# Convolution pieces in a queue beside a matrix product, a state-space stream in smaller pieces, and another division of PSUM

## The chip, the cores and the metric

The kernel runs on one core of a Trainium2 chip. Its engines work from queues of their own, each in order: TensorE (PE for its products, PEld for its weight loads), VectorE (DVE), ScalarE (ACT), GpSimd (POOL) and SyncE (SP), which here issues nearly all DMAs. The metric is the device time of one execution in microseconds (us), the median of several runs.

## The reference

Two blocks follow each other, with 2048 tokens of width 1024. The first holds attention, a short convolution and a recurrent time mix. The second, in which the change lies, projects tokens and 256 context tokens with one matrix, and mixes them by a pooling branch, a state-space stream (SSD) and a gated delta-rule stream (GDN), each in two directions over chunks of 64 tokens; a product, a router and 16 experts come behind. Cut to what matters:

```
pc, pl = split(h_ctx @ w_in), split(h_lat @ w_in)           # the second input product
# SSD: xbc = silu(conv5(xbc) + b);  xs, B, C = split(xbc);  a = decay of each step
y_intra = ((C @ B^T) * decay) @ (xs * dt)                   # within a chunk
states  = (B * exp(a_last - a))^T @ (xs * dt)               # of a chunk
s       = s * chunk_decay + states                          # from chunk to chunk
y_inter = (C * exp(a)) @ s_start
y       = rms_norm((y_f + y_b + d_skip * xs) * silu(z))
# GDN: qkv = silu(conv5(qkv));  tm = inverse(I + strict_lower((k*beta) @ k^T * decay))
u, w    = tm @ (v * beta), tm @ (k * beta * exp(g))
v_new   = u - w @ s;  o = (q*exp(g)) @ s + attn @ v_new;  s = s * g_end + k_end^T @ v_new
```

## The kernel before

`Mid.run` holds the second block up to its output product. In `In2.run` the input product goes over jobs of 128 columns. A job has for every 512 tokens 24 matmuls (three for each of eight pieces of the inner dimension, `mm3`, line 66), then a copy out of PSUM (line 1160) and, for the parts gate and z, four transposes (line 1166). It runs twice: over the first 1024 tokens and the context, and over the other 1024 tokens ("the second run", 25 jobs: dab 1, qkv 9, pool 2, xbc 7, gate 3, z 3).

Beside the second run stand, each emitted whole or by shares between jobs: `Decay.run` (decay tables, some vector work), `ConvG.group` for nine groups of GDN channels (per group five pieces: four taps on VectorE, line 1209, a last multiplication, line 1212, transposes, line 1220; then norms and transposes back), `Pool.run` (eight pieces: sums on GpSimd, line 1390, on VectorE, line 1392, one matmul, line 1398, a copy by ScalarE, line 1400), and `ConvS.run`, the convolution of SSD, seven groups for each stretch of tokens in `CSP`.

Then comes the mixed stage. `Gdn.run` is 18 steps, a new one every `GDN_EVERY` = 15 rounds of `timed`, its front part `GDN_LEAD` = 16 rounds earlier. A step is: front (`ld`, `gram`), the inverse (`TriInv`: first part on VectorE, lines 256 to 296, second part five rounds of small products `tri`, line 318, each copied out of PSUM before the next), and `back` (`big` twice, line 1767, then `chain`, lines 1793 and 1796, which carries the state). Each round of GDN also calls `feed(RATE3)`, which draws the other stream: the rest of `ConvS` and then `Ssd.run`, first backwards (d = 1), then forwards (d = 0), by pairs of chunks. A chunk ("unit" below) is four matmuls: `y` from the state (line 1916) and `st` (line 1922), with the state scaled by GpSimd (line 1927) and `st` added by VectorE (line 1928). Forwards, a pair also has the products within its chunks ("intra part"): `g`, two `ld` (line 1950) with exponentials by ScalarE (line 1951), products of these by VectorE and GpSimd (lines 1952, 1954, 1958), `i` (line 1963), the sums and the gate (line 98).

The program's text gives priorities only: a scheduler orders every engine's queue by them and by when it believes operands and buffers free. PSUM has eight banks; in the mixed stage three tiles of two banks are shared by all of GDN's products, and two of one bank by the other stream:

```
pg, pq = k.psum(eg, "gp", 3, **R), k.psum(eg, "sp", 2, **L)
RATE3 = 0.35
```

Of the kernel before, what the change touches and what calls it, by code (L numbers as in the profile page):

```python
# [1125 lines left out]
class In2:  # L1126
# [22 lines left out]
    def block(self, wts, segs, hh, hl, dst=None, tok=None):  # L1149
# [4 lines left out]
        for c0, n, p0 in segs:  # L1154
            for u in range(0, n, 512):
                un = min(512, n - u)
                ps = self.pp.tile([128, 512], F32, tag="ps", name="ps")
                k.mm3(ps[:m, :un], [(wh[:, c], wl[:, c], hh[:, c, c0 + u:c0 + u + un], hl[:, c, c0 + u:c0 + u + un]) for c in (ROT if m == 36 else range(8))])
# [12 lines left out]
    def run(self, order, segs, hh, hl):  # L1171
# [15 lines left out]
        for j, (part, i, _, sg, kw) in enumerate(jobs):  # L1187
            nxt = self.weights(*jobs[j + 1][2]) if j + 1 < len(jobs) else None
            self.block(w, sg, hh, hl, **kw)
            w = nxt  # L1190
            yield part, i

# [43 lines left out]
class ConvG(Conv):  # L1236


    def __init__(self, k, a, es, p2, gT, gtm, psf, psf2, **kw):
# [4 lines left out]
        self.cw = self.weights(a["gdn_conv_w_2"][0], 9, w1)  # L1244

    def group(self, g):
# [21 lines left out]
        for p0, n in PIECES:  # L1268
            s0 = p0 + (4 if p0 == T else 0)
            y = self.taps(self.cw[:, g], None, pad[:, s0:s0 + n + 4], n)  # L1270
            t, m = p0 // 128, n // 128
            self.turn(tm[:, t:t + m].rearrange("p t c -> p (t c)"), lambda j: y[:, j * 128:j * 128 + 128], m)
            if g >= 6:
                continue
            sq = wp.tile([128, 8, 64], F32, tag="sq", name="sq")[:, :2 * m]
            tv = th[:, 2 * t:2 * t + 2 * m]
            G_.tensor_tensor(out=sq, in0=tv, in1=tv, op=ALU.mult)
            V.tensor_reduce(out=ss[:, 2 * t:2 * t + 2 * m], in_=sq, axis=AX.X, op=ALU.add)
# [3 lines left out]
        rs = k.rstd(wp, ss, 36, 1.0, 1e-6, "l2")  # L1282
        if g < 3:
            V.tensor_scalar(out=rs, in0=rs, scalar1=0.125, scalar2=None, op0=ALU.mult)
        for p0, n in PIECES:
            t, m = p0 // 128, n // 128
            tv = th[:, 2 * t:2 * t + 2 * m]
            G_.tensor_tensor(out=tv, in0=tv, in1=bc(rs[:, 2 * t:2 * t + 2 * m].unsqueeze(2), [128, 2 * m, 64]), op=ALU.mult)
            y = wp.tile([128, 512], F32, tag="yn", name="yn")
            self.turn(y[:, :n], lambda j: tm[:, t + j, :], m, self.psf2)  # L1290
            nc.sync.dma_start(self.gT[g * 128:g * 128 + 128, p0:p0 + n], y[:, :n])
        if g >= 3:
            store(0, 0, 18)


class ConvS(Conv):
# [12 lines left out]
    def run(self, pieces):  # L1309
        for p0, n in pieces:  # L1310
            for g in range(7):
                self.piece(g, p0, n)
                yield

    def piece(self, g, p0, n):
# [14 lines left out]
        if g < 5:  # L1330
            m = n // 128
            tm = wp.tile([128, 4, 128], F32, tag="tm", name="tm")[:, :m]
            self.turn(tm.rearrange("p t c -> p (t c)"), lambda j: y[:, j * 128:j * 128 + 128], m)
            nc.sync.dma_start(self.sst[p0:p0 + n, g * 128:g * 128 + 128].rearrange("(t p) c -> p t c", p=128), tm)
# [125 lines left out]
class Decay:  # L1460


    def __init__(self, k, a, es, p2, **kw):
        nc = k.nc
        self.k, self.a, self.p2, self.nc = k, a, p2, nc
        self.srow = k.dram([NCH, 12, 64], "srow")
# [7 lines left out]
    def run(self, psf, **kw):  # L1474
# [5 lines left out]
        with ExitStack() as e2:  # L1480
# [36 lines left out]
            dt = softplus(nc, wp, xr[:, 0:2, :], [NP, 2, 256], "sp")  # L1517
            beta = wp.tile([NP, 256], F32, tag="beta", name="beta")
# [30 lines left out]
            v.tensor_tensor(out=e2b, in0=e2v[:, 1, :], in1=beta, op=ALU.mult)  # L1549

# [11 lines left out]
            for n, src in back.items():  # L1562
                if n not in self.cols and n not in self.g:
                    continue
                ps = psf("t")
# [24 lines left out]
            nc.sync.dma_start(gt.rearrange("p s c d h -> p (s c d h)"), gdc.rearrange("c d -> (c d)").partition_broadcast(128))  # L1590
            for c in range(4):
                self.by_step(self.g["gdc"], c, gt[:, :, c].rearrange("p s d h -> p d s h"))

# [265 lines left out]
class Ssd:  # L1859


    def __init__(self, k, a, m, dec, es, bcT, sst, ztok, stok, psf, **kw):
# [4 lines left out]
        self.w2 = k.pool(es, "ss2", 2, **kw)  # L1867
        self.yb = [k.dram([128, 384], f"yb{p}") for p in range(16)]
# [12 lines left out]
    def run(self):  # L1881
# [12 lines left out]
        for d in (1, 0):  # L1894
            S = None
            order = ([16, 17] if d == 0 else [17, 16]) + (list(range(16)) if d == 0 else list(range(15, -1, -1)))
            for p in order:
                lat = p < 16
                t0 = p * 128
                xb = w2.tile([128, 640], F32, tag="xb", name="xb")  # L1900
                nc.sync.dma_start(xb, self.sst[t0:t0 + 128, :])
                xs = h6(xb[:, 0:384])
                xw = w2.tile([128, 6, 64], F32, tag="xw", name="xw")
                G_.tensor_tensor(out=xw, in0=xs, in1=bc(dec.col("sw", p, d).unsqueeze(2), [128, 6, 64]), op=ALU.mult)
                if lat:
# [6 lines left out]
                for i, u in enumerate((0, 1) if d == 0 else (1, 0)):  # L1912
                    rows = slice(u * 64, u * 64 + 64)
                    if lat:
                        for g in range(2):
                            nc.tensor.matmul(py[rows, g * 192:g * 192 + 192], bct[:, 2 + g, rows], S[:, g * 3:g * 3 + 3, :], start=True, stop=True)
                        if i == 1:
# [13 lines left out]
                if not lat:  # L1931
                    continue
# [544 lines left out]
```

## Time and profile before

| what | value |
|---|---|
| median of three runs | 4551.71 us (4546.35 to 4559.96) |
| profiled execution | 4546.18 us, its span 4544.4 us |
| busy in the span | PE 85%, PEld 71%, DVE 61%, ACT 43%, POOL 30% |
| mean granted clock of TensorE | 0.927 of full speed |
| second run of the input product | from about 2240 to 2683 us of the span |
| mixed stage | from about 2690 to 3497 us |

Busy time is the sum of an engine's instructions; PE's are modelled at their ends, so that a busy share near 90% does not mean that no time is left. A wait row names the instruction that waited and what released it.

### The profile page before, as it was taken

How to read it: one execution, taken by the hardware profiler on the slowest of the kernel's cores; microseconds unless marked ns; L12 is line 12 of the kernel's file. 1: busy time of each engine (PE TensorE's matmuls, PEld its weight loads, DVE VectorE, ACT ScalarE, POOL GpSimd, SP SyncE). 2: the span in 40 equal slices, each digit the busy share in tenths (PEclk: the TensorE clock that was granted, in tenths of full speed). 3: DMA queues.
4: the chain of work that ended last, by engine and by line, in shares of the span. 5: the costliest groups of instructions: out<-in, count | busy, mean ns of one | idle time of the engine just before them, and what ended most of it. 6: DMA issues, size and time to landing. Idle time of an engine off the chain costs nothing. (4 is left out here: it accounts for less than half of the span.)

```text
span 4544.4 us, 69094 instructions
## 1 busy us (share of the span) xinstructions
PE 3884.3 (85%) x25852; PEld 3231.2 (71%) x25852; DVE 2791.8 (61%) x5608; ACT 1960.8 (43%) x3984; POOL 1341.9 (30%) x1138
## 2 busy tenths in 40 slices
PE   7899999899788879899987858888885993799993
PEld 5688777677577767788765647777775783689993
DVE  7644555664588855323289776666776446866664
ACT  3134434343678742233336545455555221244442
POOL 2222222322311112221145444445553431011110
PEclk9999999899899989999989989998888996899997
DMA  6722322421412133334444654433333534577776
GB/s 224 233 85 83 96 91 85 120 69 57 124 48 69 49 107 130 128 104 142 109 112 143 171 155 121 130 99 99 105 109 111 175 119 135 176 232 234 232 228 203
DMA packets 551829, 595.65 MB, mean 131 GB/s; under 512 B 98310, under 2 KB 435378, under 8 KB 551494
## 3 DMA queue, kind: packets, MB, share of 16 engines
q1 hardware_dynamic: 538182, 547.17, 39.1%
q0 software_dynamic: 13312, 44.06, 4.0%
q8 instruction: 205, 3.36, 0.3%
q14 instruction: 130, 1.06, 0.1%
HBM read 426.62 MB, written 164.20 MB: 130 GB/s over the span
## 5 line engine op out<-in xcount | busy, mean ns | idle before, releaser
L66 PE MATMUL ps<-hh,wh 128*128 128x512 f32 (+2 forms) x1992 | 806.4, 405 | 4.9 <-ACT st L1160 3.4
L66 PE MATMUL ps<-hh,wl 128*128 128x512 f32 (+2 forms) x1992 | 783.4, 393 | 0.0
L66 PE MATMUL ps<-hl,wh 128*128 128x512 f32 (+2 forms) x1992 | 783.3, 393 | 0.0
L73 POOL TENSOR_TENSOR wl<-raw,wh 128x1024 fp32r<-128x1024 f32 (+1 forms) x136 | 320.8, 2361 | 820.3 <-ACT wh L72 785.8
L72 ACT CAST wh<-raw 128x1024 fp32r<-128x1024 f32 (+2 forms) x236 | 320.0, 1365 | 443.1 <-PE g L66 156.7
L66 PEld LDWEIGHTS ps<-hh,wh 128*128 128x128 f32 (+1 forms) x1992 | 380.4, 191 | 89.4 <-issue 6.1
L66 PEld LDWEIGHTS ps<-hh,wl 128*128 128x128 f32 (+1 forms) x1992 | 379.4, 190 | 85.1 <-issue 2.5
L66 PEld LDWEIGHTS ps<-hl,wh 128*128 128x128 f32 (+1 forms) x1992 | 381.3, 191 | 77.5 <-issue 2.2
L1209 DVE SCALAR_TENSOR_TENSOR y<-pad,cw,y 128x512 f32<-128x512 f32 (+2 forms) x348 | 263.6, 794 | 103.7 <-ACT y L1207 93.2
L66 PE MATMUL g<-xh,wh 128*128 128x256 f32 x1024 | 291.3, 286 | 17.2 <-ACT xh L2323 17.2
L66 PE MATMUL g<-xl,wh 128*128 128x256 f32 x1024 | 290.3, 284 | 1.6 <-DVE idx L2305 1.6
L66 PE MATMUL g<-xh,wl 128*128 128x256 f32 x1024 | 291.3, 285 | 0.0
L73 DVE TENSOR_TENSOR wl<-raw,wh 128x2048 fp32r<-128x2048 f32 (+1 forms) x100 | 225.1, 2263 | 105.2 <-ACT wh L72 104.8
L66 PE MATMUL o<-wh,mh 128*128 128x512 f32 x512 | 207.5, 406 | 12.7 <-DMA mraw<-mixT 12.7
L801 DVE TENSOR_REDUCE nm<-s 128x1 f32<-128x512 f32 (+3 forms) x320 | 186.0, 604 | 51.6 <-PE s L796 33.0
L2390 POOL DMA_INDIRECT x<-y,idx x32 | 63.3, 1980 | 520.1 <-DVE y L2388 452.8
L66 PEld LDWEIGHTS g<-xh,wh 128*128 128x128 f32 x1024 | 195.0, 191 | 18.5 <-ACT xh L2323 17.9
L66 PE MATMUL o<-wl,mh 128*128 128x512 f32 x512 | 206.3, 403 | 0.4 <-POOL wl L73 0.4
L66 PE MATMUL o<-wh,ml 128*128 128x512 f32 x512 | 204.2, 399 | 1.2 <-POOL ml L73 1.2
L66 PEld LDWEIGHTS g<-xl,wh 128*128 128x128 f32 x1024 | 194.8, 190 | 2.4 <-DVE idx L2305 1.8
L809 ACT ACTIVATE P<-s,mn 128x512 f32<-128x512 f32 (+3 forms) x288 | 181.0, 640 | 32.7 <-DVE mn L806 32.3
L66 PEld LDWEIGHTS g<-xh,wl 128*128 128x128 f32 x1024 | 194.2, 190 | 0.0
(671 smaller groups left out, 8988.8 us busy)
## 6 DMA issues: line engine op xcount, KB each, us to landing
raw<-in_w_in_dram SPq DMA_DIRECT2D x114, 512.0 KB
pT<-st SPq DMA_DIRECT2D x132, 256.0 KB
raw<-in_exp_w_gate_dram SPq DMA_DIRECT2D x32, 1024.0 KB
raw<-in_exp_w_up_dram SPq DMA_DIRECT2D x32, 1024.0 KB
raw<-in_exp_w_down_dram SPq DMA_DIRECT2D x32, 1024.0 KB
w<-in_ada_w_dram SPq DMA_DIRECT2D x48, 512.0 KB
xt<-in_x_dram SPq DMA_DIRECT2D x40, 512.0 KB
p<-st SPq DMA_DIRECT2D x72, 256.0 KB
```

The source lines that it names most:

```text
L66: self.nc.tensor.matmul(ps, a, b, start=(first and i == 0), stop=(last and i == n - 1))
L72: nc.scalar.copy(hi, src)
L73: (lo_eng or nc.vector).tensor_tensor(out=lo, in0=src, in1=hi.bitcast(F32), op=ALU.subtract)
L801: V.tensor_reduce(out=nm[:, m, c:c + 1], in_=ps[:, :w], axis=AX.X, op=ALU.max, negate=True)
L809: A.activation(P[m][:, c * 512:c * 512 + w], x, AF.Exp, bias=mn, accum_out=sm[:, m, c:c + 1])
L1209: V.scalar_tensor_tensor(out=y, in0=pad[:, j:j + n], scalar=w[:, j:j + 1], in1=y, op0=ALU.mult, op1=ALU.add)
L2390: G_.indirect_dma_start(out=self.x2, out_offset=bass.IndirectOffsetOnAxis(ap=idx[j], axis=0), in_=y, in_offset=None, compute_op=ALU.add)
```

## The change

- `In2.block` yields after each half of its 24 matmuls. The second run takes its parts as dab, qkv, xbc, pool, gate, z.
- A class `Work` holds generators first in, first out. At each such yield it is asked for `CVR` = 1.25 pieces. `Decay.run` (now ten pieces), `ConvG.group` (now eight pieces a group, the transposes two pieces behind the taps, norms and transposes back drawn along with the next group) and the `ConvS` piece go into it. `Pool` is drawn at a fifth of a piece per yield, from the second pool job on.
- `ConvS` makes the transposes of a piece after the taps of the next.
- `Ssd.run` yields after each unit instead of each pair, and four times more in the intra part; the `st` products of a unit are issued with the unit before it; the gate's Tanh is issued a piece ahead of its use.
- `RATE3` is 0.63, and for the first 16 rounds three times that.
- PSUM: two tiles of two banks for GDN's `gram`, `big` and `ld`; four of one bank for `tri`, `chain` and the other stream.

```diff
+                for i in range(0, 8, 4):
+                    k.mm3(ps[:m, :un], [(wh[:, c], wl[:, c], hh[:, c, c0 + u:c0 + u + un], hl[:, c, c0 + u:c0 + u + un]) for c in ROT[i:i + 4]], i == 0, i == 4)
+                    yield
...
+class Work:
+    def __call__(self, n):
+        self.due += n
+        while self.due >= 1:
+            if not self.gens:
+                self.due = 0.0
+                return
+            try:
+                next(self.gens[0])
+                self.due -= 1
+            except StopIteration:
+                self.gens.pop(0)
...
+        for j in range(8):
+            for f, i in ((taps, j), (turned, j - 2), (squares, j - 3)):
+                if 0 <= i < 5:
+                    f(i)
+            if self.after:
+                self.after.pop(0)()
+            yield
...
+                if S is not None:
+                    G_.tensor_tensor(out=Sn, in0=S, in1=bc(dec.sdc[:, p * 2 + u, d * 6:d * 6 + 6].unsqueeze(2), [128, 6, 64]), op=ALU.mult)
+                if lat:
                     for g in range(2):
+                        nc.tensor.matmul(py[rows, g * 192:g * 192 + 192], bct[:, 2 + g, rows], S[:, g * 3:g * 3 + 3, :], start=True, stop=True)
+                ps = states.pop(j)
...
+                    V.tensor_tensor(out=Sn, in0=Sn, in1=h6(ps), op=ALU.add)
+                S = Sn
+                if j + 1 < len(units):
+                    inputs(j + 1)
                 yield
...
-                    for part, i in i2.run(("dab", "qkv", "pool", "xbc", "gate", "z"), [(0, 1024, 1024)], *hB):
+                    for x in i2.run(("dab", "qkv", "xbc", "pool", "gate", "z"), [(0, 1024, 1024)], *hB):
+                        if x is None:
+                            work(CVR)
+                            if pool:
+                                pool(POOL / 4)
+                            continue
...
-                pg, pq = k.psum(eg, "gp", 3, **R), k.psum(eg, "sp", 2, **L)
+                pg, pq = k.psum(eg, "gp", 2, **R), k.psum(eg, "sp", 4, **L)
...
-                         lambda n: pg.tile([128, 1024], F32, tag="b", name=n), **R)
+                         lambda n: psf(n) if n in ("tri", "chain") else pg.tile([128, 1024], F32, tag="b", name=n), **R)
...
-                for _ in gd.run():
-                    feed(RATE3)
+                for i, _ in enumerate(gd.run()):
+                    feed(RATE3 * (RAMP if i < GDN_LEAD else 1))
...
-RATE3 = 0.35
+RATE3, RAMP = 0.63, 3.0
```

Where the instructions go, first TensorE at the opening of the mixed stage, from the last `gram` of the first two fronts to the first `tri`. Before:

```order
L1739 MATMUL gram<-kq,kbd 128x128 x12
L318 MATMUL tri<-d,xt 64x64 x24
L318 MATMUL tri<-y_23501,dt 64x64 x24
L318 MATMUL tri<-d,xt 64x64 x12
L318 MATMUL tri<-dt,y_23501 64x64 x12
```

and now, where the rows `y` and `st` go on in turn until the first `tri`:

```order
L1828 MATMUL gram<-kq,kbd 128x128 x6
L1260 MATMUL t<-ident,y 128x128 x6
L2015 MATMUL st<-xw,xb 128x192 x8
L1817 MATMUL ld<-er_23517,el_23515 128x512
L1817 MATMUL ld<-er_23517,el_23515 128x256
L2029 MATMUL y<-S,bct 64x192 x2
L2015 MATMUL st<-xw,xb 128x192 x2
L318 MATMUL tri<-d,xt 64x64 x24
```

In all 42 rows' worth of `st` (21 units) and 32 of `y` now stand ahead of the first `tri`, and 58 of `st` (29 units) ahead of the first `chain`; before none did.

VectorE at the same place, from the first inverse's last operations on (`db`, line 296, is what the first `tri` waits for; `S<-S,st` the sum of a unit). Before, the inverse of the next step follows at once:

```order
L288 TENSOR_REDUCE tn<-tmp 128x8x8
L296 STREAM_TRANSPOSE db<-da 128x512 x2
L258 STREAM_TRANSPOSE xb<-xc 128x512
L260 TENSOR_TENSOR xp<-xb 128x256
L270 TENSOR_SCALAR tn<-xp 128x4
```

and now

```order
L288 TENSOR_REDUCE tn<-tmp 128x8x8
L1961 TENSOR_SCALAR ng<-ng 128x384
L296 STREAM_TRANSPOSE db<-da 128x512
L2034 TENSOR_TENSOR S<-S,st 128x384
L296 STREAM_TRANSPOSE db<-da 128x512
L2034 TENSOR_TENSOR S<-S,st 128x384
L258 STREAM_TRANSPOSE xb<-xc 128x512
```

The first sum of a unit stands behind the inverse of step 0, and the others among the inverse of step 1.

TensorE in a later step, where an intra part lies. Before:

```order
L1946 MATMUL g<-bct 64x64 x4
L1950 MATMUL ld<-er_24412,el_24410 128x384
L318 MATMUL tri<-d,xt 64x64 x9
L1950 MATMUL ld<-er_24412,el_24410 128x384
L318 MATMUL tri<-d,xt 64x64 x3
```

and now

```order
L2060 MATMUL g<-bct 64x64 x4
L2064 MATMUL ld<-er_23912,el_23910 128x384 x2
L318 MATMUL tri<-y_23501,dt 64x64 x12
L318 MATMUL tri<-d,xt 64x64 x12
L318 MATMUL tri<-dt,y_23501 64x64 x12
```

The two `ld` of an intra part follow each other, and a `tri` group is no longer cut between them.

## Rows read from the trace of the kernel before

**Rows 1.** Busy time by engine: window, its length, PE, PEld, DVE, ACT, POOL.
```profile
2240.00:2583.00 343.00, 283.17 (x1255) 220.37 (x1253) 292.13 (x557) 173.49 (x274) 146.99 (x161) 0.92 0.49 142
...
2976.00:3359.00 383.00, 330.41 (x3474) 276.38 (x3474) 264.21 (x517) 208.21 (x428) 203.59 (x183) 0.87 0.37 103
```

**Rows 2.** Timeline of ScalarE, 2570 to 2665 us: copies of the pool pieces.
```profile
2584.87 0.69 ACT L1400 ACTIVATE y<-t,psc 128x512 f32<-128x512 f32 x1 [0.87 <-PE t L1398]
...
2656.80 0.69 ACT L1400 ACTIVATE y<-t,psc 128x512 f32<-128x512 f32 x1
```

**Rows 3.** Groups by line and form, 2300 to 2720 us: busy, mean ns.
```profile
L1209 DVE SCALAR_TENSOR_TENSOR y<-pad,cw,y 128x512 f32<-128x512 f32 x160 | 138.8, 885 | 0.2
```

**Rows 4.** Waits of TensorE, 2690 to 2800 us: total, times, longest.
```profile
PE tri L318 <- ACT d L311: 26.3, 1, 26.3
```

**Rows 5.** Timeline of VectorE, 2684 to 2730 us: the first inverse.
```profile
2703.36 9.77 DVE L273 TENSOR_TENSOR tmp<-tn,xp 128x16 f32<-128x16 f32 x1
...
2724.58 0.71 DVE L296 STREAM_TRANSPOSE db<-da 128x512 f32<-128x512 f32 x1 [0.97 <-ACT da L294]
...
2726.74 0.18 DVE L273 TENSOR_TENSOR tmp<-tn,xp 128x16 f32<-128x16 f32 x1
```

**Rows 6.** Timeline of GpSimd, the same stretch.
```profile
2704.01 1.48 POOL L1748 TENSOR_TENSOR kv<-kv,dsge 128x768 f32<-128x768 f32 x1
...
2711.63 1.46 POOL L1746 TENSOR_TENSOR U<-kv,dsge 128x768 f32<-128x768 f32 x1
```

**Rows 7.** Timeline of TensorE: the first `chain` of a step.
```profile
2752.31 0.83 PE L1793 MATMUL chain<-ubd,U 128*128 128x128 f32 x6
...
2790.88 0.50 PE L1793 MATMUL chain<-ubd,U 128*128 128x128 f32 x3
...
2975.71 0.50 PE L1793 MATMUL chain<-ubd,U 128*128 128x128 f32 x3
...
3358.69 0.50 PE L1793 MATMUL chain<-ubd,U 128*128 128x128 f32 x3
...
3397.50 0.72 PE L1793 MATMUL chain<-ubd,U 128*128 128x128 f32 x5
...
3432.90 0.50 PE L1793 MATMUL chain<-ubd,U 128*128 128x128 f32 x3
```

**Rows 8.** Lines 1922 and 1963 in windows 2791:2976 (first) and 2976:3359.
```profile
L1922 PE MATMUL st<-xw,xb x152: 322/323/686, 2794.4 to 2973.6; 64*128 64x192 f32 x152
...
L1922 PE MATMUL st<-xw,xb x112: 322/323/686, 2998.3 to 3356.6; 64*128 64x192 f32 x112
...
L1963 PE MATMUL i<-xb,mbd x168: 221/275/475, 2992.3 to 3345.5; 128*128 128x64 f32 x168
```

**Rows 9.** Lines 1927, 1928 and 1904, 2690 to 3500 us: ns minimum, median, maximum.
```profile
L1927 POOL TENSOR_TENSOR S<-S,sdcb x70: 820/830/1694, 2771.6 to 3354.8; 128x384 f32<-128x384 f32 x70
...
L1928 DVE TENSOR_TENSOR S<-S,st x70: 515/553/556, 2772.5 to 3357.0; 128x384 f32<-128x384 f32 x70
...
L1904 POOL TENSOR_TENSOR xw<-xb,dcsw x36: 830/841/1551, 2769.2 to 3333.8; 128x384 f32<-128x384 f32 x36
```

**Rows 10.** Waits of TensorE, 2800 to 3420 us.
```profile
PE ld L1950 <- ACT E L1951: 18.5, 10, 2.6
...
PE tri L318 <- ACT y L1802: 15.1, 8, 2.7
...
PE i L1963 <- DVE mbd L1958: 7.5, 4, 2.7
```

**Rows 11.** Waits of VectorE, 2800 to 3420 us.
```profile
DVE S L1928 <- PE st L1922: 28.0, 26, 4.1
...
DVE z L98 <- ACT yb L97: 17.2, 10, 3.4
DVE E L1952 <- ACT E L1951: 16.6, 10, 3.2
```

**Rows 12.** Tile `big`, 2690 to 3500 us: a copy of it, ns minimum, median, maximum.
```profile
L1774 ACT ACTIVATE wbd<-big x72: 463/486/488, 2744.7 to 3484.0; 64x384 f32<-64x384 f32 x72
```

More of the change, by code (lines that the diff above doesn't have):

```diff
@@ L1188, in run, with __init__, add, late @@
             nxt = self.weights(*jobs[j + 1][2]) if j + 1 < len(jobs) else None
-            self.block(w, sg, hh, hl, **kw)
+            yield from self.block(w, sg, hh, hl, **kw)
             w = nxt
             yield part, i
+class Work:
+    def __init__(self):
+        self.gens, self.due = [], 0.0
+    def add(self, gen):
+        self.gens.append(gen)
+    def late(self, make):
+        def gen():
+            yield from make()
+        self.add(gen())
+    def __call__(self, n):
[9 more added lines that the diff above has]
+                self.gens.pop(0)
+    def until(self, dec):
+        while not dec.done:
+            self(1)
+    def rest(self):
+        for g in self.gens:
+            drain(g)
+        self.gens = []
 class Conv:
@@ L1281, in group, with flush @@
             return
[L1282 to L1291, printed above, removed]
-        if g >= 3:
-            store(0, 0, 18)
+        self.after = [roots]
+        for j in range(6):
+            self.after.append(lambda j=j: ((j < 5 and scaled(j)), (j > 0 and out(j - 1))))
+        if g >= 3:
+            self.after.append(lambda: store(0, 0, 18))
+    def flush(self):
+        while self.after:
+            self.after.pop(0)()
+            yield
 class ConvS(Conv):
@@ L1896, in run, with load @@
             order = ([16, 17] if d == 0 else [17, 16]) + (list(range(16)) if d == 0 else list(range(15, -1, -1)))
-            for p in order:
-                lat = p < 16
+            units = [(p, u) for p in order for u in ((0, 1) if d == 0 else (1, 0))]
+            loaded, states = {}, {}
+            def load(p):
                 t0 = p * 128
-                xb = w2.tile([128, 640], F32, tag="xb", name="xb")
+                xb = self.w3.tile([128, 640], F32, tag="xb", name="xb")
                 nc.sync.dma_start(xb, self.sst[t0:t0 + 128, :])
[L1902 to L1905, printed above, removed]
+                bct = el = er = None
+                if p < 16:
                     bct = w2.tile([128, 4, 128], F32, tag="bct", name="bct")
@@ L1930, in run, with inputs @@
-                yield
+                loaded[p] = [xb, None, bct, el, er]
+            def inputs(j):
+                p, u = units[j]
+                if j % 2 == 0:
+                    if p not in loaded:
+                        load(p)
+                    xw = loaded[p][1] = w2.tile([128, 6, 64], F32, tag="xw", name="xw")
+                    G_.tensor_tensor(out=xw, in0=h6(loaded[p][0][:, 0:384]), in1=bc(dec.col("sw", p, d).unsqueeze(2), [128, 6, 64]), op=ALU.mult)
+                xb, xw = loaded[p][:2]
+                rows = slice(u * 64, u * 64 + 64)
+                ps = states[j] = self.psf("st")[:, 0:384]
+                for g in range(2):
+                    nc.tensor.matmul(ps[:, g * 192:g * 192 + 192], xb[rows, 384 + g * 128:512 + g * 128], xw[rows, g * 3:g * 3 + 3, :], start=True, stop=True)
@@ L2040, in run @@
                     cv = ConvG(k, a, ec, self.p2, self.gT, self.gtm, psf, lambda n: pn.tile([128, 512], F32, tag="t", name=n), **L)
[L2041 to L2056 removed]
+                    work, pool = Work(), None
@@ new lines, in run @@
+                    for x in i2.run(("dab", "qkv", "xbc", "pool", "gate", "z"), [(0, 1024, 1024)], *hB):
[3 more added lines that the diff above has]
+                                pool(POOL / 4)
+                            continue
+                        part, i = x
+                        if part == "dab":
+                            work.add(dec.run(psf, **L))
+                        elif part == "qkv":
+                            work.add(cv.group(i))
+                        elif part == "xbc" and i == 6:
+                            work.add(cv.flush())
+                            work.late(lambda: ConvS(k, a, ec, self.p2, self.bcT, self.sst, psf, **L).run(CSP[1]))
+                        elif part == "pool" and i == 1:
+                            work.until(dec)
+                            pool = Feed(Pool(k, a, ec, self.p2, self.mix2T, psf, **L).run())
```

135 lines of the change are left out of this document (80 added, 55 removed).

## The prediction

> **What bounds the kernel now.** I read the busy times by stage first, then what ends TensorE's and VectorE's waits in each stage, then the pace of the steps.
>
> In the second run of the input product VectorE is the bound, not TensorE: of 343 us it is busy 292.1, 85%, and TensorE's weight loads 220.4, 64% [rows 1]. A tap of 512 columns takes 885 ns [rows 3], and a conv piece has four of them. The reader is to see that whatever order the pieces have, VectorE's sum stays.
>
> At the opening of the mixed stage TensorE stands still once for 26.3 us, until ScalarE has copied the first inverse [rows 4]. That inverse ends on VectorE at 2724.58 + 0.71 [rows 5].
>
> In the mixed stage nobody is full: from 2976 to 3359 us the weight loads are busy 72%, VectorE 69%, ScalarE 54%, GpSimd 53% [rows 1]. The pace is read from the first `chain` of each step [rows 7]. With only GDN left in the queues, a step takes 3432.90 - 3397.50 = 35.4 us. The four steps from 2790.88 to 2975.71 with the backward SSD stream take 46.2 each, the eight from there to 3358.69 with the forward stream 47.9. So the other stream costs 10.8 to 12.5 us per step on top, though no engine is full: it stands in the same in-order queues, and GDN waits behind its waits. Its prices follow. Four `st` records are a unit, so 152 are 38 units in the four steps [rows 8]: (184.8 - 4 x 35.4) / 38 = 1.14 us each. The eight steps have 28 units and, at 12 `i` records each, 14 intra parts: (383.0 - 8 x 35.4 - 28 x 1.14) / 14 = 4.9 us each.
>
> The mixed stage's 86% of matmul time against 72% of weight loads [rows 1] is also where a page bears: the Trainium skill, "Perfetto Trace Analysis", section "Identifying the Most-Contended Engine", says that matmul busy time is a bad measure of headroom and weight-load time a good one. By matmul time 53 us could at most be won in these 383, by weight loads 107; the steps of 35.4 with two thirds of the present work agree with the second.
>
> **The change, part by part.** The sum is made against the profiled execution's 4546.2 us (span 4544.4); the median, 4551.7, stands 5.5 above, within the runs' own 13.6. A difference under 0.3%, about 14 us, can't be told from none.
>
> *The queue of convolution pieces: 0 us.* It removes and adds no work. In the order of TensorE the ninth GDN group's transposes come behind the 20th of the 25 jobs, before as now, since the scheduler had already spread the groups; with VectorE the bound, that stretch stays. Behind it the `ConvS` transposes now all come before the 21st job, and the pool products one per 24 matmuls in the last four. The seven `ConvS` pieces, about five vector operations of 885 ns each, 31 us, then stand ahead of the pool chain and not among it. That chain took 2656.80 - 2584.87 over seven intervals, 10.3 us a piece [rows 2]; undisturbed I take 7.4. The last product comes at about 2583 + 31 + 7 x 7.4 = 2666, behind which only one batch of 24 matmuls stands, some 15 us earlier than now for the fronts of GDN. But about 17 us of taps of the last stretches of tokens now come behind the first front on VectorE's queue, ahead of the first inverse. So the first inverse ends where it did. Bounds: the earlier front kept whole, -15; the pool chain at its present pace, 2583 + 31 + 72, +20.
>
> *Drawing more often at first: +14 us.* In VectorE's order the sums of the units come behind the inverse of step 0, and 21 units stand on TensorE's queue ahead of the first `tri`. A unit's chain is GpSimd's 0.83 and VectorE's 0.55 us, and every second one has another 0.84 on GpSimd [rows 9]: 1.38 to 1.80 us, so 29 to 38 us for 21. I take 38, since the inverse of step 1 stands between the sums. The wait of 26.3 us, before as long as the inverse, is thus filled, but the first `tri` starts 38 us later. Of the 29 units ahead of the first `chain`, eight more are within that step, 9 us, and some four more than before stand in the next: 38 + 9 + 4 = 51 us late at the second step. 33 units fewer are left from there: 33 x 1.14 = 38 us back. Net +14 (rounded up). Bounds: the whole wait recovered, -26; nothing of the units' price given back, since they had hidden behind GDN's own waits, +40.
>
> *Smaller pieces and products ahead: -46 us.* What they take away can be named. TensorE waited 18.5 us for ScalarE before the second `ld`, because both `ld` shared the two tiles of one bank, and 7.5 us at `i` [rows 10]: with four tiles the `ld` follow each other. That is 26 us in order in front of GDN. VectorE waited 28.0 us for `st`, which is now made a unit ahead, 17.2 for the Tanh and 16.6 for the exponentials [rows 11], 61.8 us in all. Such a wait costs only if a GDN operation stands behind it that could have run; VectorE is idle for 31% of the stretch anyway. I take a third, 20 us. 26 + 20 = 46. Bounds: 0, if GDN's own latencies show instead, and 26 + 62 = 88. More than the stream's remaining price can't come back: 33 x 1.14 + 16 x 4.9 = 116 us.
>
> *PSUM: +10 us.* GDN's wide tiles fall from three to two. A `big` tile is emptied by four copies of 0.49 us [rows 12], 1.9 us, and the tile after next has to wait for it; two such per step are 0 to 3.8 us. The next product lies between, so I take 1 us per step, 17 us over 17 steps. Against it, `tri` waited 15.1 us for the copy of a `chain` tile [rows 10], and now has four tiles to rotate through, two of which the other stream holds much of the time: half, 7 us, back. Bounds: -15 and 17 x 3.8 = +65.
>
> Sum: 0 + 14 - 46 + 10 = -22, so 4546.2 - 22 = **4524 us**.
>
> **The rivals.**
>
> *The other stream hides wholly.* If the waits fall on nobody, half of the remaining 116 us goes, not 46, and the two tiles and the opening cost what I say: 14 - 70 - 15, and with more of the units hidden in the first steps about -76, 4470 us. For it speaks that no engine passes 72% [rows 1]; against it that GDN's inverse is five rounds from TensorE to a copy and back, at which any foreign instruction in the queue delays.
>
> *Slower: two wide tiles.* If each step pays 3 us for them, 51, with 26 of the 46 recovered: 14 - 26 + 51 = +39, 4585 us. It decides from 2.6 us per step on: there the 32 us that the other terms leave, and the 10 counted, are used up. For it: six of GDN's wide tiles per step come within one short stretch, `big`, `gram`, `big`, `gram`, `big`, `big`. Against it: the wait row for `big` and `gram` is not among the long ones now.
>
> *The change doesn't do what it says.* The scheduler decides the order; in the second run it hardly moved. If it does so in the mixed stage as well, since it fills a wait by what is ready, 4546 us. Against it: the `ld` pairs and the 21 units did move.
>
> *GpSimd holds VectorE.* In rows: a vector product of 16 elements took 9.77 us, and the next of its kind 0.18 [rows 5]; it ended when a run of GpSimd operations from 2704.01 on ended [rows 6]. The opening now has 31 more GpSimd operations (21 states, 10 inputs of 0.83 us) beside the inverse of step 1. If each of some 28 keeps a vector operation waiting so long, 23 us are added: 4547 us. The Trainium skill, "SBUF — State Buffer", section "SBUF: two separate sides", says that GpSimd and a vector operation with two SBUF inputs take one port pair in turns, the loser blocked for the whole instruction; this trace agrees with the 9.77 us. Against it: the sum of a unit reads PSUM, and its longest is 556 ns [rows 9].
>
> **How the numbers follow.** My forecast 0.38, on its own 4500 to 4549; the stream hidden 0.25; slower by the tiles 0.20; no effect 0.10; GpSimd 0.07. Faster by over 0.3% are 0.29 of the first and the second: 0.54. Within 0.3% are 0.09 of the first and the last two: 0.26. Slower 0.20. The range leaves out about a tenth at either end: 4462 to 4582 us.
>
> **What would show it.** The queue: `big` and `gram` aside, VectorE's last GDN tap still at about 2580 us, and the last pool copy at 2660 to 2680. The opening: the first `tri` at 2755 to 2770, the wait of 26.3 us gone. The pieces: no wait of `ld` for its exponential, less than 5 us of VectorE's for `st`, and steps of about 44 us. PSUM: waits of `big` and `gram` for copies under 25 us. I am wrong if the steps stay at 47, if they fall under 41, or if the first `tri` doesn't move.

## The result and the profile after

The changed kernel is slower: 4578.93 us, median of nine runs (4552.32 to 4587.73), against 4550.24 (4542.43 to 4560.17) for the kernel before; the ratio is 1.0051, with a 95% interval of 1.0037 to 1.0065. The forecast was 4524, faster. The profiled execution took 4552.32 us and is the fastest of the nine; a second profile of the same kernel (below, again) took 4577.67 and stands for the typical one. Both are read here.

Busy times by stage of the first profile (columns as in [rows 1]):

```profile
2240.00:2583.00 343.00, 284.18 (x1264) 221.29 (x1262) 293.20 (x556) 175.38 (x276) 142.24 (x159) 0.92 0.49 141
2976.00:3359.00 383.00, 323.67 (x3714) 271.62 (x3713) 262.20 (x533) 219.39 (x451) 190.19 (x170) 0.91 0.37 100
```

VectorE's sum in the second run is the same as in [rows 1], 293.2 against 292.1. TensorE through the opening and the steps, same profile:

```profile
2681.51 2.77 PE L1828 MATMUL gram<-kq,kbd 128*128 128x128 f32 x12
...
2730.19 3.09 PE L2015 MATMUL st<-xw,xb 64*128 64x192 f32 x16 [14.77 <-DVE mid L283]
...
2770.91 0.92 PE L2015 MATMUL st<-xw,xb 64*128 64x192 f32 x4
2771.75 0.86 PE L2029 MATMUL y<-S,bct 128*64 128x192 f32 x4
...
2773.59 1.61 PE L318 MATMUL tri<-d,xt 64*64 64x64 f32 x48
...
2803.63 1.50 PE L1882 MATMUL chain<-ubd,U 128*128 128x128 f32 x12
2848.68 0.94 PE L1882 MATMUL chain<-ubd,U 128*128 128x128 f32 x6
...
3360.26 0.66 PE L1882 MATMUL chain<-ubd,U 128*128 128x128 f32 x4
...
3489.08 0.39 PE L1882 MATMUL chain<-ubd,U 128*128 128x128 f32 x2
```

Against [rows 7] the first `chain` is 51 us late, the second 58. The steps then win nearly all of it back: the `chain` of the fourteenth step was at 3358.69 before and is now at 3360.26. The 26.3 us that the first `tri` waited [rows 4] are gone, but other waits stand there (TensorE, 2680 to 2840 us):

```profile
PE t L1260 <- DVE y L1252: 15.8, 4, 7.0
PE st L2015 <- DVE mid L283: 14.8, 1, 14.8
PE st L2015 <- POOL xw L2010: 6.9, 4, 4.5
```

and VectorE shows why. Its convolution of the last tokens now runs ahead of the first inverse and through it:

```profile
2721.02 1.65 DVE L1249 SCALAR_TENSOR_TENSOR y<-pad,cw,y 128x256 f32<-128x256 f32 x1
...
2723.49 0.41 DVE L1252 SCALAR_TENSOR_TENSOR y<-th,y 128x256 f32<-128x256 f32 x1
...
2735.74 0.70 DVE L296 STREAM_TRANSPOSE db<-da 128x512 f32<-128x512 f32 x1
```

The units need that convolution. By the profile GpSimd goes on when its last piece is through, and only then makes `xw`, the first input of a unit:

```profile
2723.96 0.74 POOL L1969 MEMSET mbd<- 128x768 f32 x1 [1.57 <-DVE y L1252]
...
2728.52 2.41 POOL L2010 TENSOR_TENSOR xw<-xb,dcsw 128x384 f32<-128x384 f32 x2
```

(The row of 14.8 us names an operation of the inverse, `mid`, as what ended the wait of `st`; the second profile puts the same wait of 14.8 us down to a DMA. Both names are inferred.) So the first `st` could not start before 2730.19, when the inverse was nearly done: it ends at 2736.44, 11 us later than in [rows 5]. The products of four units come at 2730.19, and the other 17 units, one behind the other from 2740.68 on, stand between the inverse and `tri`.

The second profile of the same program, the same place:

```profile
2687.03 2.64 PE L1828 MATMUL gram<-kq,kbd 128*128 128x128 f32 x12
...
2744.42 1.64 PE L2015 MATMUL st<-xw,xb 64*128 64x192 f32 x4 [5.82 <-POOL xw L2010]
2745.99 1.54 PE L2029 MATMUL y<-S,bct 128*64 128x192 f32 x4
...
2794.10 2.83 PE L318 MATMUL tri<-d,xt 64*64 64x64 f32 x48
...
2826.16 1.50 PE L1882 MATMUL chain<-ubd,U 128*128 128x128 f32 x12
...
3515.01 0.39 PE L1882 MATMUL chain<-ubd,U 128*128 128x128 f32 x2
```

`st` and `y` take 1.64 and 1.54 us here, and 0.92 and 0.86 in the first profile. Busy times of that stretch, first profile, then second (last three columns: granted clock, DMA share, GB/s):

```profile
2740.00:2747.00 7.00, 6.32 (x19) 4.00 (x20) 4.42 (x12) 0.00 (x0) 2.32 (x4) 0.52 0.09 19
2747.00:2773.00 26.00, 23.13 (x111) 14.90 (x111) 16.76 (x31) 2.28 (x4) 18.52 (x22) 1.00 0.68 207
```

```profile
2740.00:2795.00 55.00, 50.58 (x148) 31.58 (x150) 25.05 (x49) 5.73 (x9) 23.92 (x29) 0.51 0.38 115
```

In one execution the units ran at 2.4 GHz from 2747 on (1.00), in the other at 1.2 GHz (0.51) all the way to the first `tri`. Of the 25 us between the two, 5.5 are there at the first `gram` already, 17 lie from there to the first `chain`, and 3 in the steps. The first `st` that waits (2740.68 and 2744.42) to `tri` is 32.9 and 49.7 us.

### The profile page after: what moved, and what is told of

Its sections match the earlier page's. It is cut to its first block, busy times and chain, and to the rows that moved or that the text cites. A ratio compares the mean times of both kernels' runs of the same rounds, so it can differ in the third digit from the quotient of the medians.

```text
span 4550.5 us, 69157 instructions
## 1 busy us (share of the span) xinstructions
PE 3875.8 (85%) x25852; PEld 3223.3 (71%) x25852; DVE 2795.6 (61%) x5608; ACT 1961.1 (43%) x3984; POOL 1338.1 (29%) x1138
## 5 line engine op out<-in xcount | busy, mean ns | idle before, releaser
L1249 DVE SCALAR_TENSOR_TENSOR y<-pad,cw,y 128x512 f32<-128x512 f32 (+2 forms) x348 | 278.3, 831 | 56.3 <-ACT y L1247 45.6
L801 DVE TENSOR_REDUCE nm<-s 128x1 f32<-128x512 f32 (+3 forms) x320 | 185.8, 604 | 51.8 <-PE s L796 32.9
L809 ACT ACTIVATE P<-s,mn 128x512 f32<-128x512 f32 (+3 forms) x288 | 180.8, 639 | 32.9 <-DVE mn L806 32.1
```

The costliest lines, as they stand in the source:

```text
L801: V.tensor_reduce(out=nm[:, m, c:c + 1], in_=ps[:, :w], axis=AX.X, op=ALU.max, negate=True)
L809: A.activation(P[m][:, c * 512:c * 512 + w], x, AF.Exp, bias=mn, accum_out=sm[:, m, c:c + 1])
L1249: V.scalar_tensor_tensor(out=y, in0=pad[:, j:j + n], scalar=w[:, j:j + 1], in1=y, op0=ALU.mult, op1=ALU.add)
```

## The experiments

All times are medians; ratios are against runs of the kernel before on the same chip, whose medians were 4553 to 4558 us. A PSUM tile of two banks is called wide here, one of one bank narrow; PSUM "as before" is three wide and two narrow tiles, "anew" the division of the change.

**again**: the changed kernel, no edit. 

> The changed kernel unaltered. The profiled execution took 4552.3 us at a mean granted clock of 0.928, the median of nine is 4578.9 at about 0.923. Theory clock: the 27 us between them are TensorE at its lower level for longer in most executions; a profile of a typical execution (4575 to 4585 us) then shows the same order and the same number of waits, with the mean clock near 0.923 and the added time in stretches of lower clock. Rival: the profiled execution is typical in clock and the spread is in waits (DMA); then a profile of 4575 to 4585 us shows clock 0.927 to 0.928.

 Measured 4579.76 us, 1.0047 (1.0030 to 1.0064), profiled at 4577.67 with clock 0.922. The rows above: the clock it is. The times of all fifteen executions of this program go the same way: the three with a mean granted clock of 0.926 to 0.928 took 4552 to 4567 us, the twelve with 0.920 to 0.924 took 4569 to 4588.

**queue_only**: the kernel before, and of the change only this, with the pieces that `Work` holds:

```diff
-                    for part, i in i2.run(("dab", "qkv", "pool", "xbc", "gate", "z"), [(0, 1024, 1024)], *hB):
+                    work, pool = Work(), None
+                    for x in i2.run(("dab", "qkv", "xbc", "pool", "gate", "z"), [(0, 1024, 1024)], *hB):
+                        if x is None:
+                            work(CVR)
```

> The kernel before with the queue of convolution pieces alone (order of parts, Work, pieces of ConvG and ConvS); mixed stage as before. Theory queue: the taps of the last stretch now stand ahead of the first inverse on VectorE (in the changed kernel it ends at 2735.7 instead of 2725.3), and TensorE's clock falls longer at the seam; 4558 to 4578 us, first chain near 2763. Rival, the prediction's term of 0: 4545 to 4556 us, and the loss lies in the mixed stage.

 Measured 4538.87, 0.9967 (0.9955 to 0.9978): faster by 15 us, so neither expectation.

```profile
2686.30 3.55 PE L1828 MATMUL gram<-kq,kbd 128*128 128x128 f32 x24
...
2718.78 1.44 PE L318 MATMUL tri<-d,xt 64*64 64x64 f32 x22 [17.72 <-ACT d L311]
...
2746.18 1.50 PE L1882 MATMUL chain<-ubd,U 128*128 128x128 f32 x12
```

The whole opening is earlier: the first `tri` by 7.5 us against the trace of before (2726.28 there), the first `chain` by 6.1 against [rows 7]. Over all profiles the first `gram` is at 2676 to 2694 us in the sixteen with the queue (mean 2684), and at 2690, 2697 and 2705 in the three without (mean 2697).

**mixed_only**: the rest of the change (`Ssd.run`, `RATE3`, `RAMP`, PSUM) on the kernel before. 

> The kernel before with the mixed stage's parts alone (state-space stream in pieces, products ahead, RATE3 0.63 with the threefold start, PSUM divided anew); second input product as before. Theory queue: the opening's loss (first tri some 38 us later, 40 to 45 at the first chain) is given back by shorter steps (44 instead of 47), so 4540 to 4556 us. Rival: the mixed stage by itself carries the loss, 4568 to 4585 us.

 Measured 4576.88, 1.0045 (1.0031 to 1.0058). The rival: the loss is all here. Its convolution ends earlier than in the changed kernel, so its units start earlier (2733 against 2741 and 2744), and of what the queue wins by itself nothing is left in the changed kernel. TensorE runs at 1.2 GHz here too (granted clock 0.50 from 2730 to 2790): all 17 units from 2733 to 2787 show `st` near 1.64 and `y` near 1.54 us.

```profile
2733.18 1.64 PE L1926 MATMUL st<-xw,xb 64*128 64x192 f32 x4 [9.08 <-POOL xw L1921]
...
2820.55 1.50 PE L1793 MATMUL chain<-ubd,U 128*128 128x128 f32 x12
```

**no_ramp** and **ramp2**: fewer draws at first.

```diff
-RATE3, RAMP = 0.63, 3.0
+RATE3, RAMP = 0.63, 1.0
```

> The changed kernel with the threefold start taken out (RAMP 1). Theory opening: 14 of the 21 units that stand ahead of the first tri leave, the first chain comes about 25 us earlier (2778), and they cost 14 x 1.14 = 16 us later: 4565 to 4573 us, 6 to 14 below the changed kernel. Rival, the units at the opening are cheap since TensorE waits there for the first inverse: 4580 to 4595 us.

 Measured 4539.43, 0.9968 (0.9955 to 0.9981): 40 us below the changed kernel, not 6 to 14.

```profile
2723.66 2.83 PE L318 MATMUL tri<-d,xt 64*64 64x64 f32 x48 [5.20 <-ACT d L311]
...
2759.25 0.94 PE L1882 MATMUL chain<-ubd,U 128*128 128x128 f32 x7
...
3468.59 0.39 PE L1882 MATMUL chain<-ubd,U 128*128 128x128 f32 x2
```

The first `tri` is 50 us ahead of the changed kernel's; no unit stands ahead of it, and 9 ahead of the first `chain`.

With `RAMP` 2.0: 

> The changed kernel with RAMP 2 instead of 3: in TensorE's order 10 units of the state-space stream stand ahead of the first tri instead of 21 (none with RAMP 1). Theory: such a unit delays the first inverse by 1.75 us where TensorE runs at 2.4 GHz and by 3.05 us where it still runs at 1.2 GHz, and gives back about 1 us later; so 10 units put the time about half way between RAMP 1 (4539) and RAMP 3 (4580): 4550 to 4566 us. Rival, the loss comes only when the units outlast the wait for the first inverse, a step and not a slope: 4537 to 4545 us.

 Measured 4551.90, 0.9999 (0.9987 to 1.0011): the slope of the theory; by the ratios 14 us for the first 10 units and 22 for the 11 that follow.

**warm**: products into a tile that nobody reads, in the changed kernel.

```diff
+                if p0 in (1408, 1792):
+                    ph = self.psf("heat")
+                    for j in range(6):
+                        nc.tensor.matmul(ph[:, 0:128], k.ident, k.ident, start=True, stop=True)
...
+            if d == 1:
+                ph = self.psf("heat")
+                for j in range(24):
+                    nc.tensor.matmul(ph[:, 0:128], k.ident, k.ident, start=True, stop=True)
             inputs(0)
```

> The changed kernel with products that nobody reads (identity by identity, 128x128): 6 behind the transposes of each piece of ConvS in the mixed stage, and 24 ahead of the first unit. They keep TensorE at work while it waits there. Theory clock: it reaches the 21 units at 2.4 GHz, these take 1.75 us each instead of 3.05, and the time falls to 4550 to 4566 us. Rival: TensorE was not the limit there, or stays at 1.2 GHz; then the products only add, 4580 to 4595 us.

 Measured 4572.44, 1.0044 (1.0031 to 1.0058): inside neither range. The median is 7 us below again's, the ratio only 0.03%, 1 us: no gain that can be told. The profile tells why. Some units run at 2.4 GHz (granted clock 0.80 over the first of these two stretches), and the clock falls in the middle of them:

```profile
2730.00:2757.00 27.00, 19.64 (x84) 12.82 (x84) 17.54 (x36) 7.70 (x11) 16.47 (x20) 0.80 0.47 142
2757.00:2785.00 28.00, 25.50 (x68) 16.21 (x68) 10.33 (x17) 2.24 (x4) 12.25 (x14) 0.51 0.41 124
```

```profile
2759.50 1.64 PE L2019 MATMUL st<-xw,xb 64*128 64x192 f32 x4 [3.22 <-POOL xw L2014]
...
2785.45 2.82 PE L318 MATMUL tri<-d,xt 64*64 64x64 f32 x48
```

After a wait of 3.22 us for `xw` every unit takes 3.05 us, and TensorE is busy 25.5 of 28.

**before_ramp**: the kernel before with the threefold start alone.

```diff
-                for _ in gd.run():
-                    feed(RATE3)
+                for i, _ in enumerate(gd.run()):
+                    feed(RATE3 * (3.0 if i < GDN_LEAD else 1))
```

> The kernel before with the threefold start alone (its own pairs, its own PSUM, RATE3 0.35): 4 units stand ahead of the first tri and 18 ahead of the first chain. Theory: the loss belongs to the start and not to the pieces, so this is slower than the kernel before by 8 to 25 us (18 units at 2 us ahead of the first chain, 1 us each given back later). Rival: the old pairs fill the wait at the opening for nothing, and it is within 5 us of the kernel before or faster.

 Measured 4559.86, 1.0008 (0.9992 to 1.0023): 4 us by the ratio, which can't be told from nothing. The start by itself is not the loss.

**no_ramp_psum3**, **queue_psum**, **psum_back**: PSUM as before or anew, each time these lines.

```diff
-                pg, pq = k.psum(eg, "gp", 2, **R), k.psum(eg, "sp", 4, **L)
+                pg, pq = k.psum(eg, "gp", 3, **R), k.psum(eg, "sp", 2, **L)
...
-                         lambda n: psf(n) if n in ("tri", "chain") else pg.tile([128, 1024], F32, tag="b", name=n), **R)
+                         lambda n: pg.tile([128, 1024], F32, tag="b", name=n), **R)
```

In no_ramp: 

> The changed kernel with RAMP 1 and PSUM divided as before (three wide tiles for all of GDN, two for the other stream). The prediction's term for PSUM is +10 us: without it 4525 to 4535 us. Rival: the four narrow tiles are what lets the pieces work (products of a unit made ahead hold one), and with two the stream blocks: 4545 to 4570 us.

 Measured 4538.28, 0.9972 (0.9961 to 0.9982), 1 us from no_ramp. The other way round in queue_only: 

> The kernel with the queue of convolution pieces alone (4539 us) and, on top, only PSUM divided anew; state-space stream and rates as before. The prediction's term: +10, so 4545 to 4555 us. Rival: no cost, 4533 to 4543 us, and the shorter steps of the changed kernel come from PSUM and not from the pieces if it falls below 4530.

 Measured 4534.17, 0.9967 (0.9953 to 0.9980), the same as queue_only. In the changed kernel, `RAMP` 3 kept: 

> The changed kernel with RAMP 3 kept and PSUM divided as before (three wide tiles for GDN, two narrow for the other stream). If the new division costs its predicted 10 us or the 16 of the pair with the pause: 4560 to 4571 us. If it costs nothing: 4575 to 4584 us. With two narrow tiles the 21 units at the opening, which hold one tile a unit ahead, could also go slower: over 4585 us.

 Measured 4540.38, 0.9970 (0.9960 to 0.9980): 39 us below the changed kernel, under every expectation. With that a table of four is full (all with the queue and the pieces):

| | RAMP 1 | RAMP 3 |
|---|---|---|
| PSUM as before | 4538, 0.9972 | 4540, 0.9970 |
| PSUM anew | 4539, 0.9968 | 4580, 1.0047 |

Neither of the two edits costs anything that can be told, and both together cost 40 us, by the ratios 36. Whether the smaller pieces are needed for that was not tried: no run has both edits with the old pairs. TensorE in psum_back:

```profile
2689.70 2.56 PE L1828 MATMUL gram<-kq,kbd 128*128 128x128 f32 x11
...
2742.36 3.05 PE L2015 MATMUL st<-xw,xb 64*128 64x192 f32 x8 [2.63 <-ACT S L2032]
2745.34 2.82 PE L318 MATMUL tri<-d,xt 64*64 64x64 f32 x48
...
2754.63 0.86 PE L2029 MATMUL y<-S,bct 128*64 128x192 f32 x4
...
2811.17 1.50 PE L1882 MATMUL chain<-ubd,U 128*128 128x128 f32 x12
...
3481.22 0.83 PE L1882 MATMUL chain<-ubd,U 128*128 128x128 f32 x6
```

The draws are the same, and by the first `chain` as many units are done (31, there 30); but 4 of them stand ahead of the first `tri` instead of 21, the others between the rounds of `tri`, and the clock is up from 2754 on (`y` 0.86). From the first `chain` to that of the last step are 670 us, against 685 and 689 in the two profiles of the changed kernel. One profile of each, with no_ramp_psum3 read from these rows:

```profile
2676.01 4.03 PE L1828 MATMUL gram<-kq,kbd 128*128 128x128 f32 x24
...
2760.32 1.50 PE L1882 MATMUL chain<-ubd,U 128*128 128x128 f32 x12
...
3464.75 0.83 PE L1882 MATMUL chain<-ubd,U 128*128 128x128 f32 x6
```

| | first `gram` to first `chain` | first to last `chain` | together |
|---|---|---|---|
| queue_only | 59.9 | 731.1 | 791.0 |
| no_ramp_psum3 | 84.3 | 704.4 | 788.7 |
| no_ramp | 81.8 | 709.3 | 791.2 |
| psum_back | 121.5 | 670.1 | 791.5 |
| the changed kernel, first profile | 122.1 | 685.5 | 807.6 |
| the changed kernel, second profile | 139.1 | 688.9 | 828.0 |

So the loss has two parts. With PSUM as before the threefold start costs 37 us at the opening and the steps give 34 back; with PSUM anew they give back only 20 to 24. And the 21 units ahead of `tri` cost the opening nothing against psum_back where the clock rises among them (122.1 and 121.5), and 17 us more where it stays at 1.2 GHz.

**split** and **tri_wide**: which part of the division it is.

```diff
-                pg, pq = k.psum(eg, "gp", 2, **R), k.psum(eg, "sp", 4, **L)
+                pg, pt, pq = k.psum(eg, "gp", 2, **R), k.psum(eg, "tp", 2, **R), k.psum(eg, "sp", 2, **L)
...
+                         lambda n: pt.tile([128, 512], F32, tag="b", name=n) if n in ("tri", "chain") else pg.tile([128, 1024], F32, tag="b", name=n), **R)
```

> The changed kernel, RAMP 3, two wide tiles for GDN, but the four narrow ones divided: two for tri and chain, two for the state-space stream. In TensorE's order 4 units then stand ahead of the first tri instead of 21, and the others between the tri. Theory, the shared set is the cause: 4535 to 4546 us. Rival, two wide tiles are the cause: 4570 to 4584 us; a share for each: 4550 to 4566 us.

 Measured 4554.37, 1.0001 (0.9986 to 1.0016): a share for each. The edit of tri_wide (not shown) puts `tri` and `chain` into the two wide tiles instead: 

> The changed kernel, RAMP 3, two wide tiles that now also take tri and chain, four narrow ones for the state-space stream alone; 4 units ahead of the first tri. Theory, the shared set is the cause: no 40 us at the opening, but tri, big, gram and chain now rotate through two tiles, which costs up to 2 us a step: 4538 to 4575 us, with the first chain at 2800 to 2812 and the steps longer than in the changed kernel. Rival, two wide tiles are the cause at the opening: first chain after 2820 and 4580 us or more.

 Measured 4556.23, 0.9998 (0.9986 to 1.0010), inside the theory's range, with the first `chain` at 2803.06; the steps, 686 us in all, are no longer than in the changed kernel. Taking `tri` out of the set that it shared with the units is worth 0.5% or 22 us (1.0047 to 1.0051 against 0.9998 to 1.0001), by either way; a third wide tile another 0.3%, 14 us. From the first `gram` to the first `chain` the two take 125 and 121 us, as psum_back does. In split it is 681 us from the first `chain` (2808.45) to the last (3489.56): 11 more than in psum_back with its three wide tiles.

**late**, **late_psum3**, **late_split**: no draws while the first inverse runs, with PSUM anew, as before, and as in split.

```diff
-                    feed(RATE3 * (RAMP if i < GDN_LEAD else 1))
+                    feed(RATE3 * (0 if GDN_LEAD <= i < 2 * GDN_LEAD else 1))
```

> The changed kernel with RAMP 1 and no draws at all in rounds 16 to 31, so that no unit of the state-space stream stands ahead of the first chain (9 with RAMP 1, 29 in the changed kernel); the units come later in the same order. Theory: a unit ahead of the first chain costs about 2 us there and 1 us later, so the first chain comes 14 to 18 us earlier than with RAMP 1 (2759) and half of that stays: 4525 to 4535 us. Rival: the units cost the same wherever they stand, 4536 to 4542 us.

 Measured 4541.84, 0.9973 (0.9963 to 0.9982), and once more: 

> The kernel with the pause in the draws and PSUM divided anew, once more. If its median against the one with PSUM as before stays 10 to 16 us higher, the division costs that; if the two come within 6 us, the first difference was that of the runs.

 4542.09, 0.9972 (0.9960 to 0.9984). The rival: nothing gained by the pause where PSUM is divided anew. With three wide tiles: 

> The same pause in the draws, with PSUM divided as before (three wide tiles, two narrow). Theory: 4523 to 4533 us, as the kernel with PSUM divided anew, since that division cost nothing in two comparisons. Rival: 4536 to 4542 us, no gain from the pause.

 4525.94, 0.9953 (0.9936 to 0.9970), and again: 

> The kernel with the pause in the draws and PSUM divided as before, once more: 4520 to 4532 us if the first time was typical, 4534 to 4542 if it was not.

 4534.98, 0.9948 (0.9931 to 0.9964), by the median the first time was better than typical, and the ratio repeats. By the ratios that is 9 to 11 us below no_ramp_psum3, and the fastest kernel of the study. And 

> The division of split with RAMP 1 and the pause in the draws: no unit ahead of the first chain. If the shared set is what made the kernel with the pause and the new division slower (4542 us) than with the old one (4526 and 4535): 4526 to 4536 us. If it is the two wide tiles: 4538 to 4545 us.

 4550.91, 0.9984 (0.9972 to 0.9996): worse than expected of either theory; two narrow tiles for each are no cure here.

## Why the prediction was wrong

**The steps that failed** are two. The term that was mis-sized most is "smaller pieces and products ahead: -46 us", which measured about 0 (below, with the other terms). The step whose mechanism was wrong is "a unit's chain is GpSimd's 0.83 and VectorE's 0.55 us ... so 29 to 38 us for 21. I take 38", with its consequence, +14 for drawing more often, and its neighbour, PSUM counted by itself at +10 as a matter of two wide tiles. Three things were wrong in that one.

The unit had the wrong bound. In the first profile a unit at the opening takes 1.82 us (2750.95 to 2772.74, twelve of them), as taken in the forecast (38 / 21 = 1.81). In the other TensorE sits at 1.2 GHz and needs 1.64 + 1.54 us less the overlap, 3.05, and is itself the limit. Sixteen units would make 20 us more; 17 were measured. The working had taken every price of TensorE from the middle of the mixed stage, though the trace of before has its wait of 26.3 us at just this place, and a granted clock of 0.50 (the third number from the end) in the wait and behind it:

```profile
2710.00:2730.00 20.00, 3.71 (x70) 3.72 (x72) 16.77 (x38) 9.18 (x15) 5.16 (x5) 0.50 0.21 61
```

The wait was not there to be filled. "The wait of 26.3 us ... is thus filled": the units need the last convolution, which stands with the inverse on VectorE. What I had placed under the queue ("about 17 us of taps ... ahead of the first inverse") belonged here: by the profile it delayed the inverse by 11 us and the first four units to 2730, the other 17 to 2740, so that units and inverse came at once. No run takes the convolution away from there by itself, so its share is not measured.

The 21 units were put down to the draws. The order shows them, but with the same draws psum_back, split and tri_wide have 4. It is the shared set of narrow tiles that puts `tri` behind the units; that a set's tiles are given out in the order in which the program is written, and the units stand first there, is the likely reason. So the term was neither drawing (0 by itself, psum_back against no_ramp_psum3) nor PSUM (0 by itself) but their product: +36 to +40, where the sum had 14 + 10. The bounds of the two, up to 40 and 65, held it. The range held the time as well, but that is no merit of the sum: the side was wrong.

**The other terms.** The queue, forecast 0 (-15 to +20): -15 by itself, its lower bound ("the earlier front kept whole"). The last pool copy came at 2664.61 and 2669.93, within the 2660 to 2680 forecast, but by luck: the first copy came at 2596.7 and 2601.5, where the working has about 2614, and a piece took 9.7 us, not 7.4. The first `gram` came 9 and 3 us earlier; in queue_only, which draws at the old rate, the inverse ends at 2720.2, 5 us before that of [rows 5], and the front is kept. In the changed kernel the units take it (mixed_only and the changed kernel end alike).

The smaller pieces, forecast -46 (0 to -88): close to 0, as no_ramp_psum3 against queue_only shows (with the higher `RATE3`, which goes with the pieces): 4538 and 4539, ratios 0.9972 and 0.9967. What was read as 46 us to be won were waits that others replaced; that is the condition of the term's own lower bound, "if GDN's own latencies show instead". In the changed kernel, 2800 to 3420 us:

```profile
PE tri L318 <- DVE y L326: 14.2, 7, 4.1
PE i L2080 <- DVE mbd L2075: 11.0, 6, 3.6
```

```profile
DVE U L1830 <- PE gram L1828: 48.5, 20, 6.8
DVE z L2084 <- ACT yb L2081: 30.0, 14, 4.2
DVE S L2034 <- POOL S L2026: 21.5, 15, 5.6
```

and before:

```profile
PE tri L318 <- DVE y L326: 15.6, 10, 3.3
```

```profile
DVE U L1741 <- PE gram L1739: 18.2, 13, 3.4
```

`ld` waits for no exponential and VectorE hardly for `st` (1.9 us), as forecast. But TensorE's wait at `i`, which was to go, grew from 7.5 [rows 10] to 11.0, VectorE's for the Tanh, which was to go, from 17.2 [rows 11] to 30.0, and its wait for GDN's `gram` from 18.2 to 48.5; the sum of a unit now waits for GpSimd, 21.5 us where it was 2.6. The wait of `tri` for VectorE, 15.6 before, stayed. (no_ramp_psum3 against queue_only: `gram` 30.4 against 19.3, the sums 35.9 for GpSimd.) TensorE's busy time from 2870 to 3300 us, no_ramp, then queue_only:

```profile
2870.00:3300.00 430.00, 370.19 (x4288) 310.77 (x4284) 286.07 (x577) 246.83 (x505) 206.30 (x190) 0.91 0.39 104
```

```profile
2870.00:3300.00 430.00, 373.26 (x3943) 309.95 (x3942) 288.55 (x563) 231.03 (x475) 221.37 (x206) 0.89 0.40 108
```

It stands idle for 60 and 57 of 430 us: the smaller pieces have not made it wait less. In no_ramp_psum3 they won 27 us from first to last `chain` (3464.75 - 2760.32 = 704.4, in queue_only 731.1), with 9 units fewer to do there, and lost 24 from the first `gram` to the first `chain`, where the 9 now stand (2760.32 - 2676.01 = 84.3, in queue_only 59.9). Where no unit stands at the opening (late_psum3), the pieces win 6 to 9 us by the ratios, at the edge of what can be told.

The Trainium skill, "Perfetto Trace Analysis", section "Identifying the Most-Contended Engine", says that headroom of TensorE is to be judged by the reached share of its peak and by weight loads, and not by matmul time. No run here bears out the weight loads, with which I had sided: by them 107 us were to be had in 383, by matmul time 53, and every order tried left TensorE idle, by matmul time, for 48 to 70 of the 430 us from 2870 to 3300 (55 before). That none of these orders found the 107 us does not show that they are not there.

PSUM, forecast +10 (-15 to +65): 0 without the start, in two pairs; 14 of the 40 with it, and 9 and 11 us by the ratios with the pause (late against late_psum3, twice; 16 and 7 by the medians). Why the third wide tile counts only in these two is not settled.

Together: -15 for the queue, about 0 for the pieces, +36 to +40 for start and PSUM make +21 to +25, against +23 by the ratio of 1.0051, where the sum had 0 - 46 + 14 + 10 = -22.

**The rivals.** "Slower by two wide tiles", 4585 with a chance of 0.20, has the right side and nearly the right time, but its price of 3 us a step was not paid: 11 to 19 us over 17 steps, about the 1 us a step of the forecast's own term. The sum of "the other stream hides wholly" does not follow from its words: half of 116 us is 58 and not 70, and PSUM at what the forecast says is +10 and not -15, so that it gives 14 - 58 + 10 = -34, 4512 us; the changed kernel is near neither. (And (32 + 10) / 17 steps are 2.5 us a step, not 2.6, in "two wide tiles".) Of "GpSimd holds VectorE" the stretch of the 17 units shows nothing: from 2737 to 2774 no vector operation of the first profile took over 1.4 us. Of what was to be shown, steps of about 44 (42.8 over the thirteen from 2803.63), the missing waits of `ld` and for `st`, and the copy waits under 25 us (13 at `big`) held; the first `tri`, forecast for 2755 to 2770, came at 2774 and 2794. That row was the one to heed.

## What to carry to other kernels

Work that was drawn forward into a wait won nothing in these runs, and it cost 36 to 40 us where its own inputs came only as the wait ended and the critical operation drew its buffers from the same set: check both before its price is counted. A wait that an edit removes counts only if no other wait takes its place: here 46 us of named waits were worth about 0. Two edits that are each free can cost 40 us together, so undo them one by one and in pairs before either is blamed. Price what TensorE does behind a long wait at the clock that the rows show behind that wait, not at the clock of the stage, and take a second profile when the profiled execution is the fastest of its runs.

## What the runs showed of the hardware

TensorE stayed at 1.2 GHz while it was busy for 50.58 of 55 us (again, granted clock 0.51), and was at 2.4 GHz from 2747 to 2773 (granted clock 1.00) in another execution of the same program with the same order. The Trainium skill, "TensorE: Matmul & The Clock Gate", section "What's actually happening", says that sustained activity lifts the clock. The trace of again does not agree for its 16 units of thin products, 64 x 192 and 128 x 192: it was at 1.2 GHz through all of them, as in mixed_only. In warm it fell among such units, where TensorE had waited 3.22 us for `xw`. In again, mixed_only and warm it rose once `tri` had begun: `y` is down to 0.86 us within 7 us of the first `tri`. What distinguishes the two executions of the changed kernel, the trace does not show. With it goes a spread of 35 us (4552 to 4588), where the kernel before has 18.
